# A hybrid SSD block on one core: two of the second norm's conditioning sums move from the scan stage into the output projection, and a chunk's own part is accumulated onto its decayed state output

## The chip, the cores and the metric

One core of a Trainium2 chip runs the whole kernel. The metric is the device time of one execution in microseconds (us); lower is better. The engines are TensorE (PE, with its weight loads as PEld), VectorE (DVE), ScalarE (ACT), GpSimd (POOL) and SyncE (SP), which issues all the transfers of this kernel from one in-order queue.

## The reference, cut to what matters

One layer of a diffusion backbone: a bidirectional Mamba-2 (SSD) mixer over 512 latent tokens that starts from the final state of 256 context tokens, then a convolutional gated FFN. Six conditioning vectors come from one vector `c` through `ada_w` (1024 x 6144): shift, scale and gate of the first norm, and the same of the second.

```python
sh1, sc1, g1, sh2, sc2, g2 = split(silu(c) @ ada_w[i] + ada_b[i], 6)
hl = rmsnorm(x, norm1_w[i]) * (1 + sc1) + sh1
oc, ol = mamba2_mixer(hc, hl, ...)
x = x + g1 * ol
x = x + g2 * conv_ffn(rmsnorm(x, norm2_w[i]) * (1 + sc2) + sh2, ...)
```

```python
# one direction of the mixer, per chunk of 128 tokens and head
y = (einsum("bcrls,bcsrp->bclrp", mix, xd)                       # the chunk's own part
     + einsum("bcln,bcrpn,bcrl->bclrp", cc, carried, exp(la_cs)))  # decayed state output
```

So `sh2` and `sc2` (parts 3 and 4 of the six) are needed only when the second norm's output is modulated, after the output projection; `g1` (part 2) is needed where that projection's result is added to `x`.

## The kernel before, in words

**Stages.** The kernel normalizes and transposes the input (until about 70 us), then works group by group over four groups of eight heads (the scan stage), then applies `w_out` (the output projection), the FFN's up projection with its convolution, and its down projection. All large weights are split into a high and a low part (`split`, line 94: ACT copies the high part, DVE subtracts it), and each product is three matmuls.

**The scan stage.** `ssm_group` (line 714) runs one group: the state passes (`advance`), and per chunk `mixing` (line 753), which loads decays (`R`), runs the DVE scan on them, adds the two directions into `M`, multiplies it with `cb`, and loads the decays to the chunk (`eb`). Per chunk two sorts of matmul follow: `pi`, the chunk's own part (eight fp32 matmuls of `xk` and `M`), and `pe`, the state output of either direction (four each). Five DVE instructions of 128x512 join them: `pe*eb` for both directions, their sum, the sum with `pi`, and the sum into `u`. `pi` and the two `pe` take one bank each of the PSUM pool `py`, which has three.

**What fills the gaps.** While group g is scanned, `blend` (line 931) interleaves "pieces" of other work in the code: the input projections of group g+1 (`proj_pieces`), gate projections with `w_z` (`gate_pieces`), and the conditioning sums (`ada_pieces`, line 843). A conditioning part has eight pieces; a piece loads 128 rows of `ada_w` (512 KB) and adds them, scaled by `silu(c)`, into a 128x1024 sum with one DVE instruction. `with_ada` puts one such piece behind each other piece, until the 24 pieces of parts 3, 4 and 2 are used up:

```python
ada = chain(ada_pieces(3, ada_acc, then=ada_to_cols), ada_pieces(4, ada_acc, then=ada_to_cols),
            ada_pieces(2, ada_acc, then=ada_bias))
```

`ada_to_cols` (line 866) sums the 128 partitions with eight small matmuls against `ones` (the tile `ada_c`); `ada_to_rows` (line 879) does so for `g1` in the output projection. All weight tiles, of `ada_w` too, go through one pool of three buffers (`wraw`, line 84); their high and low parts through another of three (`wsp`).

**The output projection.** `token_matmul` (line 969) takes 16 tiles of `w_out` (`raw_o`, split into `hi_o` and `lo_o`) against `u` (`uh`, `ul`) into eight PSUM banks (`o`); the last four tiles are kept, and for them the tokens are done block by block (i = 0 to 3). Behind a block come `add_and_norm` (line 1033: `ot`, the sum with `x`, the norm `xn`) and `modulated` (line 1048: transposes into the same banks, scale and shift into `h2hi` and `h2lo`). Three tiles of the FFN's up weights (`raw_a`, `raw_g`, `raw_a`) are loaded and split in advance.

**Order.** Outside the stretches that are held in program order, a scheduling layer places the instructions of each engine's queue; each engine then runs its queue in order.

Of the kernel before, what the change touches and what calls it, by code (L numbers as in the profile page):

```python
# [10 lines left out]
F32 = mybir.dt.float32  # L11
# [3 lines left out]
ALU = mybir.AluOpType  # L15
# [51 lines left out]
def hybrid_kernel(  # L67
# [646 lines left out]
    def ssm_group(g):  # L714
# [82 lines left out]
        for ch in range(NC):  # L797
            cs = slice(ch * P, (ch + 1) * P)
            M, eb = nxt
            pi = bank(py, f"pi{g}{ch}").rearrange("p (j l) -> p j l", l=P)  # L800
            for j in range(4):
                for q in range(2):
                    h = 2 * j + q
                    mm(pi[64 * q:64 * q + 64, j], xk[:, ch, h * HD:(h + 1) * HD], M[:, 4 * q + j])
            t = eb
            for dr, S in ((0, Sf), (1, Sb[ch])):
                pe = bank(py, f"pe{g}{ch}{dr}").rearrange("p (j l) -> p j l", l=P)
                for j in range(4):
                    mm(pe[:, j], S[:, j * P:(j + 1) * P], cT[:, cs])
                V.tensor_tensor(pe if dr else t[:, 0], pe, eb[:, dr], op=ALU.mult)  # L810

            V.tensor_tensor(t[:, 0], t[:, 0], pe, op=ALU.add)
            V.tensor_tensor(pi, pi, t[:, 0], op=ALU.add)
            us = u[:, 4 * g:4 * g + 4, cs]
            V.tensor_tensor(us, us, pi, op=ALU.add)
            if ch < NC - 1:
                nxt = mixing(ch + 1)
                yield
                Sf = advance(Sf, 0, ch, f"Sf{g}_{ch + 1}")
            yield  # L820
# [44 lines left out]

    def ada_to_cols(part, a):
        pc = bank(pj, f"ada_c{part}")
        for m in range(KD):
            mm(pc[:, m:m + 1], a[:, m * P:(m + 1) * P], ones)
        V.tensor_tensor(modc[:, part, :, 0], pc[:, :KD], prmB[:, KD * part:KD * part + KD], op=ALU.add)  # L870
        if part == 4:
            V.scalar_tensor_tensor(h2s, modc[:, 4, :, 0], 1.0, n2w, ALU.add, ALU.mult)
# [5 lines left out]

    def ada_to_rows(a, name):
        parts = split(a, name)  # L880
        for h in range(2):
# [22 lines left out]
    def with_ada(pieces):  # L904
        for p_ in pieces:
            yield p_
            yield from islice(ada, 1)

    ada = chain(ada_pieces(3, ada_acc, then=ada_to_cols), ada_pieces(4, ada_acc, then=ada_to_cols),
                ada_pieces(2, ada_acc, then=ada_bias))  # L910
    phases = [proj_pieces(0)] + [with_ada(p_) for p_ in (
        proj_pieces(1), proj_pieces(2), chain(proj_pieces(3), gate_pieces(0)),
        chain(gate_pieces(1), gate_pieces(2)), gate_pieces(3))] + [ada]
    ends = []
# [31 lines left out]
    finish_phase(0)  # L946
    for g, ratio in enumerate((0.6, 0.6, 0.9, 0.6)):
        blend(ssm_group(g), g + 1, ratio)
# [16 lines left out]
    h2hi = x2p.tile([P, KD, LAT], F32R, tag="h2hi", name="h2hi")  # L965
    h2lo = x2p.tile([P, KD, LAT], F32R, tag="h2lo", name="h2lo")
    Q.dma_start(x2, x.rearrange("(i p) d -> p i d", p=P))
# [49 lines left out]
    with tc.tile_pool(name="uo", bufs=5) as uo, tc.tile_pool(name="wlo", bufs=4) as wlast:  # L1017
# [11 lines left out]
        last_of = lambda: [wlast.tile([P, 1024], F32R, tag=n, name=f"{n}_last") for n in ("whi", "wlo")]  # L1029
        get_w = lambda k, last: wrows(w_out, k, f"o{k}", None, last_of if last else None)  # L1030
        xns = {}
# [45 lines left out]
        for i, o in token_matmul(acc8, 16, get_w, get_u, 3, 4, 512, up_ahead):  # L1077
            add_and_norm(i, o)
            if 0 < i < 3:
                modulated(i - 1, acc8[i - 1])  # L1080
# [20 lines left out]
    def gate2():  # L1101
        yield from stream(ada_pieces(5, g2r, True, ada_bias), 0)
        ada_to_rows(g2r, "g2b")
        yield
# [111 lines left out]
```

## Time and profile before

| | us |
|---|---|
| median of 3 runs | 971.22 (969.15 to 972.81) |
| the profiled execution's own time | 972.9 |
| its span, first to last instruction | 971.1 |
| TensorE busy in the span | 902.7 |
| VectorE busy in the span | 717.2 |

The span is what the views below divide; the profiled execution took 1.8 us more than its span, and lies within 0.2% of the median. "Busy" of TensorE is a sum over matmuls whose ends are modelled, so it includes the time that a matmul is stretched by a lower clock.

### The profile page before, as it was taken

The numbers are of one execution on the slowest core, as the hardware profiler recorded it, in microseconds if no ns is written. First come the engines' busy times: TensorE is split into PE (matmuls) and PEld (weight loads), VectorE is DVE, ScalarE is ACT, GpSimd is POOL, SyncE is SP. The second block draws the span as 40 slices with busy tenths as digits, with TensorE's granted clock in tenths as the row PEclk, the third lists the DMA queues.
The fourth block names the chain that finished last, engine by engine and source line by source line (L and its number), as shares of the span: only waits on it lengthen the run. The fifth ranks groups of instructions, "written<-read, shape, count | busy, mean of one in ns | idle before, by whom it ended". The sixth has DMA issues, their size and how long they took to land.

```text
span 971.1 us, 12065 instructions
## 1 busy us (share of the span) xinstructions
PE 902.7 (93%) x4595; PEld 736.8 (76%) x4595; DVE 717.2 (74%) x961; ACT 344.8 (36%) x523; POOL 301.6 (31%) x223
## 2 busy tenths in 40 slices
PE   7999868788889979899999999999989999999996
PEld 6688756666667767687888888888868888888885
DVE  5689989888977889657754457878898888843336
ACT  6463332222213322334344336444544333321223
POOL 2133249454535632414100004002400000453446
PEclk9999888899999999899999999999999999999998
DMA  9923364435554365533434350334534333323322
GB/s 313 292 57 101 109 145 119 112 94 155 169 144 120 98 184 141 141 88 104 135 121 140 109 152 1 112 112 148 161 107 120 87 107 92 105 87 92 104 65 87
DMA packets 137891, 119.70 MB, mean 123 GB/s; under 512 B 23245, under 2 KB 118249, under 8 KB 137833
## 3 DMA queue, kind: packets, MB, share of 16 engines
q1 hardware_dynamic: 137833, 118.93, 42.3%
q8 instruction: 36, 0.59, 0.3%
q14 instruction: 22, 0.18, 0.1%
HBM read 116.49 MB, written 2.43 MB: 122 GB/s over the span
## 4 chain that ended last, share of the span: by engine, by line
PE 51%; DVE 24%; DMA 12%; issue 9%; POOL 2%; ACT 2%; SPq 1%; DVEq 0%; ACTq 0%; POOLq 0%
PE d L59 12%; PE o L59 8%; PE pz L59 8%; PE pg L59 7%; PE pa L59 6%; DMA R<-da_d 5%; DMA adaw<-in_ada_w_dram 4%; DVE M L59 3%; DVE ada_acc L59 3%; DVE R L59 2%; DVE et L59 2%; PE pl_x L59 2%; DVE fc L59 2%; SPq L59 1%; DVE cv_lx L59 1%
## 5 line engine op out<-in xcount | busy, mean ns | idle before, releaser
L59 DVE SCALAR_TENSOR_TENSOR fc<-pa,prmC,fc 128x441 f32<-128x441 f32 (+2 forms) x176 | 121.4, 693 | 13.3 <-ACT fc L59 9.8
L59 POOL TENSOR_TENSOR raw_d<-raw_d,g2r 128x1024 f32<-128x1024 f32 x22 | 56.1, 2556 | 176.1 <-DMA raw_d<-in_ffn_w_down_dram 159.8
L59 PE MATMUL pa<-h2lo,hi_a 128*128 128x512 f32 (+1 forms) x192 | 71.5, 373 | 0.8 <-POOL h2lo L59 0.5
L59 PE MATMUL pa<-h2hi,lo_a 128*128 128x512 f32 (+1 forms) x192 | 71.5, 372 | 0.6 <-DVE lo_a L59 0.6
L59 PE MATMUL pa<-h2hi,hi_a 128*128 128x512 f32 (+1 forms) x192 | 71.5, 373 | 0.1
L59 PE MATMUL pg<-h2hi,lo_g 128*128 128x512 f32 (+1 forms) x184 | 70.1, 381 | 0.4 <-DVE lo_g L59 0.4
L59 PE MATMUL pg<-h2hi,hi_g 128*128 128x512 f32 (+1 forms) x184 | 70.1, 381 | 0.0
L59 PE MATMUL pg<-h2lo,hi_g 128*128 128x512 f32 (+1 forms) x184 | 69.9, 380 | 0.0
L59 DVE TENSOR_TENSOR lo_d<-raw_d,hi_d 128x1024 fp32r<-128x1024 f32 x18 | 34.2, 1902 | 42.9 <-ACT hi_d L59 42.9
L59 PE MATMUL pl_x<-hhi,hi_x 128*128 128x512 f32 x128 | 54.2, 425 | 4.0 <-DVE cv_cx L59 4.0
L59 POOL TENSOR_TENSOR M<-M,tok_m 64x512 f32<-64x512 f32 x32 | 41.9, 1310 | 51.1 <-DMA M<-em_d 43.2
L59 DVE TENSOR_TENSOR_SCAN R<-R,dg 128x1024 f32<-128x1024 f32 x16 | 40.2, 2516 | 23.7 <-DMA R<-da_d 17.2
L59 PE MATMUL pl_x<-hhi,lo_x 128*128 128x512 f32 x128 | 53.4, 419 | 0.0
L59 PE MATMUL pz<-hhi,lo_z 128*128 128x512 f32 x128 | 52.7, 412 | 0.0
L59 PE MATMUL pz<-hhi,hi_z 128*128 128x512 f32 x128 | 52.7, 412 | 0.0
L59 PE MATMUL pl_x<-hlo,hi_x 128*128 128x512 f32 x128 | 51.6, 405 | 0.0
L59 PE MATMUL pz<-hlo,hi_z 128*128 128x512 f32 x128 | 51.2, 400 | 0.0
L59 POOL TENSOR_TENSOR dg<-diag,tok_dt 128x1024 f32<-128x1024 f32 x16 | 34.4, 2148 | 42.7 <-DVE R L59 41.7
L59 POOL TENSOR_TENSOR xw<-xk,tok_w 128x512 f32<-128x512 f32 x24 | 35.1, 1468 | 34.1 <-PE ps_Sf L59 17.1
L59 PE MATMUL d<-lo_d,fhi 128*128 128x512 f32 x144 | 44.5, 389 | 0.0
L59 PE MATMUL d<-hi_d,flo 128*128 128x512 f32 x144 | 44.5, 389 | 0.0
L59 PE MATMUL d<-hi_d,fhi 128*128 128x512 f32 x144 | 43.6, 389 | 0.0
(339 smaller groups left out, 2410.6 us busy)
## 6 DMA issues: line engine op xcount, KB each, us to landing
adaw<-in_ada_w_dram SPq DMA_DIRECT2D x32, 512.0 KB, 3.8
raw_a<-in_ffn_w_up_dram SPq DMA_DIRECT2D x22, 512.0 KB, 4.6
raw_g<-in_ffn_w_up_dram SPq DMA_DIRECT2D x22, 512.0 KB, 4.0
raw_d<-in_ffn_w_down_dram SPq DMA_DIRECT2D x22, 512.0 KB, 3.7
adaw<-in_ada_w_dram SPq DMA_DIRECT2D x8, 1024.0 KB
raw_x<-in_ssm_w_in_dram SPq DMA_DIRECT2D x16, 512.0 KB, 3.9
R<-da_d SPq DMA_DIRECT2D x32, 256.0 KB, 4.4
eb<-e_d SPq DMA_DIRECT2D x32, 256.0 KB, 5.1
```

Of the source, the lines that this page charges most:

```text
L59: ins = f(*a, **kw)
```

## The change

Two things change. First, in a chunk the state outputs are multiplied by their decays before the chunk's own part is computed: the forward one in place in its PSUM bank, the backward one into `eb`; the eight `pi` matmuls then accumulate (`start=False`) onto the forward bank, and two DVE sums follow instead of three. A chunk takes two banks of `py` instead of three. Second, parts 3 and 4 leave the scan stage: their pieces are called from `get_w` of the output projection, one behind each `w_out` tile, into a buffer that `h2lo` takes over later, and `ada_to_cols` writes its columns into a bank of block 0 once block 1's matmuls are issued. Part 2's eight pieces move to the last group's scan, whose ratio rises from 0.6 to 1.2; the FFN's gate row (`gate2`) is split one piece earlier than it is multiplied.

```diff
-            pi = bank(py, f"pi{g}{ch}").rearrange("p (j l) -> p j l", l=P)
+            pes = []
+            for dr, S in ((0, Sf), (1, Sb[ch])):
+                pe = bank(py, f"pe{g}{ch}{dr}").rearrange("p (j l) -> p j l", l=P)
+                for j in range(4):
+                    mm(pe[:, j], S[:, j * P:(j + 1) * P], cT[:, cs], start=(j == 0))
+                V.tensor_tensor(eb[:, 1] if dr else pe, pe, eb[:, dr], op=ALU.mult)
+                pes.append(pe)
+            pi = pes[0]
             for j in range(4):
                 for q in range(2):
                     h = 2 * j + q
-                    mm(pi[64 * q:64 * q + 64, j], xk[:, ch, h * HD:(h + 1) * HD], M[:, 4 * q + j])
-            t = eb
-            for dr, S in ((0, Sf), (1, Sb[ch])):
-                pe = bank(py, f"pe{g}{ch}{dr}").rearrange("p (j l) -> p j l", l=P)
-                for j in range(4):
-                    mm(pe[:, j], S[:, j * P:(j + 1) * P], cT[:, cs])
-                V.tensor_tensor(pe if dr else t[:, 0], pe, eb[:, dr], op=ALU.mult)
-            V.tensor_tensor(t[:, 0], t[:, 0], pe, op=ALU.add)
-            V.tensor_tensor(pi, pi, t[:, 0], op=ALU.add)
+                    mm(pi[64 * q:64 * q + 64, j], xk[:, ch, h * HD:(h + 1) * HD], M[:, 4 * q + j], start=False)
+            V.tensor_tensor(pi, pi, eb[:, 1], op=ALU.add)
...
-    ada = chain(ada_pieces(3, ada_acc, then=ada_to_cols), ada_pieces(4, ada_acc, then=ada_to_cols),
-                ada_pieces(2, ada_acc, then=ada_bias))
-    phases = [proj_pieces(0)] + [with_ada(p_) for p_ in (
-        proj_pieces(1), proj_pieces(2), chain(proj_pieces(3), gate_pieces(0)),
-        chain(gate_pieces(1), gate_pieces(2)), gate_pieces(3))] + [ada]
+    ada = ada_pieces(2, ada_acc, then=ada_bias)
+    phases = [proj_pieces(0), proj_pieces(1), proj_pieces(2), chain(proj_pieces(3), gate_pieces(0)),
+              with_ada(chain(gate_pieces(1), gate_pieces(2))), with_ada(gate_pieces(3)), ada]
...
-    for g, ratio in enumerate((0.6, 0.6, 0.9, 0.6)):
+    for g, ratio in enumerate((0.6, 0.6, 0.9, 1.2)):
...
-    h2lo = x2p.tile([P, KD, LAT], F32R, tag="h2lo", name="h2lo")
+    ada34 = x2p.tile([P, 4, D], F32, tag="h2lo", name="ada34")
...
-        get_w = lambda k, last: wrows(w_out, k, f"o{k}", None, last_of if last else None)
+        mod2 = stream(chain(ada_pieces(3, ada34[:, 0]), ada_pieces(4, ada34[:, 1])), 0)
+        def get_w(k, last):
+            w = wrows(w_out, k, f"o{k}", None, last_of if last else None)
+            next(mod2, None)
+            return w
...
             add_and_norm(i, o)
+            if i == 1:
+                for part in (3, 4):
+                    ada_to_cols(part, ada34[:, part - 3], acc8[0][1][:, 32 * part:])
+                h2lo = x2p.tile([P, KD, LAT], F32R, tag="h2lo", name="h2lo")
             if 0 < i < 3:
                 modulated(i - 1, acc8[i - 1])
```

The engines' queues move in three places that matter. On VectorE, in the scan of the third group where its second chunk is prepared, the queue before holds five `ada_acc` instructions and the two small ones that end part 3 and 4 (`modc`, `h2s`):

```order
L59 TENSOR_TENSOR modc<-ada_c_2791,prmB 128x8
L59 TENSOR_SCALAR ada_acc<-adaw_2788,s_col 128x1024
L59 TENSOR_TENSOR M_2899<-M_2899,cb_2541 128x1024
L59 SCALAR_TENSOR_TENSOR R_3017<-R_3017,dg_3022 128x1024
L59 SCALAR_TENSOR_TENSOR h2s<-modc,prmA 128x8
L59 SCALAR_TENSOR_TENSOR ada_acc<-adaw_2916,s_col,ada_acc 128x1024
L59 SCALAR_TENSOR_TENSOR cv_cx_2865<-pc_x_2815,prmA,cv_cx_2865 128x255
L59 TENSOR_TENSOR Sb_0_2678<-Sb_0_2678,ps_Sb_0_2674 128x512
L59 SCALAR_TENSOR_TENSOR ada_acc<-adaw_3033,s_col,ada_acc 128x1024
L59 SCALAR_TENSOR_TENSOR cv_cx_2865<-pc_x_2815,prmA,cv_cx_2865 128x255
L59 SCALAR_TENSOR_TENSOR ada_acc<-adaw_3133,s_col,ada_acc 128x1024
```

At the same place (the third group's second and third chunk) the changed queue has only the scan's and the projections' own instructions:

```order
L59 TENSOR_TENSOR Sb_1_2600<-Sb_1_2600,ps_Sb_1_2596 128x512
L59 TENSOR_TENSOR pe_2742<-pe_2742,eb_2525 128x512
L59 SCALAR_TENSOR_TENSOR cv_lx_2737<-pl_x_2707,prmA,cv_lx_2737 128x511 x2
L59 TENSOR_TENSOR lo_c_2962<-raw_c_2781,hi_c_2961 128x1024
L59 SCALAR_TENSOR_TENSOR cv_cx_2837<-pc_x_2787,prmA,cv_cx_2837 128x255 x2
L59 TENSOR_TENSOR Sb_0_2673<-Sb_0_2673,ps_Sb_0_2669 128x512
L59 TENSOR_TENSOR M_2942<-R_2943 64x8x64 x2
L59 TENSOR_TENSOR M_2942<-M_2942,cb_2475 128x1024
L59 SCALAR_TENSOR_TENSOR R_3064<-R_3064,dg_3069 128x1024
```

What moved: the first `ada_acc` of the scan stage now stands in the last gate projections of the third group's scan, and eight are left there instead of 24.

On VectorE again, at the end of the output projection, ahead of the first block's `ot`, the queue before is:

```order
L59 TENSOR_TENSOR wlo_last<-raw_o_4513,whi_last 128x1024
L59 TENSOR_TENSOR lo_o_4472<-raw_o_4469,hi_o_4471 128x1024
L59 TENSOR_TENSOR wlo_last<-raw_o_4523,whi_last 128x1024
L59 SCALAR_TENSOR_TENSOR ul_4530<-u,prmA,uh_4529 128x512
L59 TENSOR_TENSOR wlo_last<-raw_o_4533,whi_last 128x1024
L59 TENSOR_TENSOR lo_a_4546<-raw_a_4543,hi_a_4545 128x1024
L59 SCALAR_TENSOR_TENSOR ul_4540<-u,prmA,uh_4539 128x512
L59 TENSOR_TENSOR lo_g_4552<-raw_g_4549,hi_g_4551 128x1024
L59 TENSOR_TENSOR lo_a_4558<-raw_a_4555,hi_a_4557 128x1024
L59 SCALAR_TENSOR_TENSOR ot_4585<-o_4087,rstd_87,ada_acc 128x512
```

and of the change:

```order
L59 TENSOR_TENSOR wlo_last<-raw_o_4451,whi_last 128x1024
L59 SCALAR_TENSOR_TENSOR ada_3966<-adaw_4457,s_col,ada_3966 128x1024
L59 TENSOR_TENSOR wlo_last<-raw_o_4464,whi_last 128x1024
L59 SCALAR_TENSOR_TENSOR ada_3966<-adaw_4470,s_col,ada_3966 128x1024
L59 SCALAR_TENSOR_TENSOR ul_4487<-u,prmA,uh_4486 128x512
L59 TENSOR_TENSOR wlo_last<-raw_o_4477,whi_last 128x1024
L59 SCALAR_TENSOR_TENSOR ada_3966<-adaw_4483,s_col,ada_3966 128x1024
L59 TENSOR_TENSOR lo_a_4493<-raw_a_4490,hi_a_4492 128x1024
L59 TENSOR_TENSOR lo_g_4499<-raw_g_4496,hi_g_4498 128x1024
L59 TENSOR_TENSOR lo_a_4505<-raw_a_4502,hi_a_4504 128x1024
L59 SCALAR_TENSOR_TENSOR ot_4532<-o_3986,rstd_87,ada_acc 128x512
```

What moved: the conditioning sums (`ada_3966`) stand between the splits of the last `w_out` tiles, and the three splits of the up weights come closer to `ot`.

On TensorE, behind the last matmul of block 1 (bank `o_4090` before, `o_3989` in the change), the queue before goes on with:

```order
L59 MATMUL o_4090<-whi_last,ul_4540 128x512
L59 MATMUL o_4087<-ident,xn_4591 128x128 x4
L59 MATMUL o_4088<-ident,xn_4591 128x128 x4
L59 MATMUL o_4091<-whi_last,uh_4509 128x512
L59 MATMUL o_4092<-whi_last,uh_4509 128x512
```

and the changed one with:

```order
L59 MATMUL o_3989<-whi_last,ul_4487 128x512
L59 MATMUL o_3987<-ones,ada_3966 128x1 x16
L59 MATMUL o_3986<-ident,xn_4538 128x128 x4
L59 MATMUL o_3987<-ident,xn_4538 128x128 x4
L59 MATMUL o_3990<-whi_last,uh_4447 128x512
L59 MATMUL o_3991<-whi_last,uh_4447 128x512
```

What moved: sixteen small matmuls of the column sums stand ahead of block 0's transposes and of block 2.

## Rows read from the trace of the kernel before

**Rows 1.** Windows: length, then PE, PEld, DVE, ACT, POOL busy, clock, DMA share, GB/s.

```profile
70.00:130.00 60.00, 52.66 (x284) 46.09 (x283) 58.01 (x97) 21.55 (x36) 16.91 (x22) 0.91 0.37 103
...
280.00:330.00 50.00, 45.88 (x280) 37.17 (x279) 35.51 (x48) 18.83 (x31) 20.87 (x17) 0.97 0.43 118
...
70.00:404.00 334.00, 285.72 (x1596) 229.57 (x1594) 287.92 (x341) 96.89 (x159) 158.53 (x115) 0.93 0.49 131
...
404.00:503.50 99.50, 99.50 (x502) 79.44 (x501) 65.71 (x81) 37.33 (x58) 21.75 (x17) 0.98 0.35 100
...
503.50:583.00 79.50, 79.50 (x360) 65.92 (x359) 37.85 (x50) 31.03 (x41) 2.20 (x2) 1.00 0.47 147
```

**Rows 2.** Waits of PE from 130 to 404 us: total, times, longest.

```profile
PE pi L59 <- DVE M L59: 8.8, 2, 6.9
PE pe L59 <- DVE u L59: 8.0, 4, 4.0
PE ps_Sb L59 <- DVE Sb L59: 6.2, 2, 5.9
PE pi L59 <- DVE eb L59: 4.4, 2, 3.3
```

**Rows 3.** DVE by line and form, 70 to 130 us: busy, mean ns, idle before.

```profile
L59 DVE SCALAR_TENSOR_TENSOR ada_acc<-adaw,s_col,ada_acc 128x1024 f32<-128x1024 f32 x4 | 7.3, 1830 | 0.0
```

**Rows 4.** The same view, 130 to 404 us.

```profile
L59 DVE TENSOR_TENSOR_SCAN R<-R,dg 128x1024 f32<-128x1024 f32 x15 | 37.1, 2476 | 21.7 <-DMA R<-da_d 15.2 <-DMA M<-em_d 3.3 <-POOL xw L59 2.4
L59 DVE TENSOR_TENSOR M<-R 64x512 f32<-64x512 f32 x28 | 32.1, 1146 | 0.3
L59 DVE SCALAR_TENSOR_TENSOR ada_acc<-adaw,s_col,ada_acc 128x1024 f32<-128x1024 f32 x17 | 31.0, 1821 | 4.0 <-DMA adaw<-in_ada_w_dram 4.0
...
L59 DVE TENSOR_TENSOR eb<-eb,pe 128x512 f32<-128x512 f32 x12 | 8.1, 675 | 0.1
...
L59 DVE SCALAR_TENSOR_TENSOR ada_acc<-ident,prmB,ada_acc 128x128 f32<-128x128 f32 x8 | 3.0, 446 | 0.0
...
L59 DVE TENSOR_SCALAR ada_acc<-adaw,s_col 128x1024 f32<-128x1024 f32 x2 | 2.1, 1060 | 0.0
```

**Rows 5.** Instructions on the tile ada_acc: ns min/median/max, first and last start.

```profile
L59 DVE SCALAR_TENSOR_TENSOR ada_acc<-adaw,s_col,ada_acc x21: 1250/1627/3518, 84.1 to 370.9; 128x1024 f32<-128x1024 f32 x21
```

**Rows 6.** PE by line and form, 130 to 404 us: busy, mean ns, idle before.

```profile
L59 PE MATMUL ada_c<-ones,ada_acc 128*128 128x1 f32 x32 | 3.9, 235 | 0.0
```

**Rows 7.** Transfers: issues, KB each, median us to landing.

```profile
adaw<-in_ada_w_dram SPq DMA_DIRECT2D x32, 512.0 KB, 3.8
...
R<-da_d SPq DMA_DIRECT2D x32, 256.0 KB, 4.4
...
raw_o<-in_ssm_w_out_dram SPq DMA_DIRECT2D x16, 512.0 KB, 4.8
...
raw_b<-in_ssm_w_in_dram SPq DMA_DIRECT2D x4, 512.0 KB, 7.2
```

**Rows 8.** Instructions on the tile raw_o: its landing times.

```profile
DMA to landing us min/median/max: 3.4/4.8/6.1
```

**Rows 9.** Timeline of DVE in the output projection, one tile of twelve.

```profile
527.40 0.75 DVE L59 SCALAR_TENSOR_TENSOR ul<-u,prmA,uh 128x512 fp32r<-128x512 f32 x1 [3.27 <-ACT uh L59]
528.34 1.23 DVE L59 TENSOR_TENSOR lo_o<-raw_o,hi_o 128x1024 fp32r<-128x1024 f32 x1 [0.19 <-ACT hi_o L59]
532.84 0.75 DVE L59 SCALAR_TENSOR_TENSOR ul<-u,prmA,uh 128x512 fp32r<-128x512 f32 x1 [3.27 <-ACT uh L59]
```

**Rows 10.** Timeline of DVE at the first block's end.

```profile
571.70 1.23 DVE L59 TENSOR_TENSOR lo_a<-raw_a,hi_a 128x1024 fp32r<-128x1024 f32 x1 [3.71 <-ACT hi_a L59]
575.83 1.41 DVE L59 SCALAR_TENSOR_TENSOR ot<-o,rstd,ada_acc 128x512 f32<-128x512 f32 x2 [2.90 <-PE o L59]
...
580.40 0.81 DVE L59 TENSOR_SCALAR xn<-x,rp_s,rp_t 128x1024 f32<-128x1024 f32 x1
```

**Rows 11.** Timeline of PE at block 1's end.

```profile
581.36 1.06 PE L59 MATMUL o<-ident,xn 128*128 128x128 f32 x8
```

More of the change, by code (lines that the diff above doesn't have):

```diff
@@ L864, in ada_pieces, with ada_to_cols @@
             yield partial(load, k), partial(run, k=k)
-    def ada_to_cols(part, a):
-        pc = bank(pj, f"ada_c{part}")
+    def ada_to_cols(part, a, pc):
         for m in range(KD):
@@ L877, in ada_bias, with ada_to_rows @@
             V.scalar_tensor_tensor(a[:, s], ident, prmB[:, KD * part + m:KD * part + m + 1], a[:, s], ALU.mult, ALU.add)
-    def ada_to_rows(a, name):
-        parts = split(a, name)
+    def ada_to_rows(a, name, parts=None):
+        parts = parts or split(a, name)
         for h in range(2):
@@ L1102, in gate2 @@
         yield from stream(ada_pieces(5, g2r, True, ada_bias), 0)
-        ada_to_rows(g2r, "g2b")
+        parts = split(g2r, "g2b")
+        yield
+        ada_to_rows(g2r, "g2b", parts)
         yield
```

## The prediction, made before the changed kernel was run

> **What bounds the kernel now.** I read the windows first, since the busy shares of the whole span average over stages with different limits. In [rows 1] the reader should compare TensorE (the first number behind the length) with VectorE (the third). From 404 to 503.5 us, the last gate projections, TensorE is busy all 99.5 us, and so it is from 503.5 to 583, the output projection (79.50 of 79.5), where VectorE has 37.85. There nothing but TensorE's own work sets the time, and VectorE work is free as long as it comes in time. From 70 to 404 us, the scan of the first three groups, it is otherwise: of 334 us TensorE has 285.72 (85.5%) and VectorE 287.92 (86.2%), and the granted clock is 0.93 on average, so part of TensorE's busy time is matmuls at 1.2 instead of 2.4 GHz. TensorE is idle there for 334 - 285.7 = 48.3 us.
>
> Next, whom it waits for: the longest waits [rows 2] all end with a VectorE instruction (`M`, `u`, `Sb`, `eb`), 27.4 us in four rows. That is a queue that runs late, and the lines of VectorE [rows 3, 4] tell with what: the scan itself, the additions into `M`, and then `ada_acc`, the conditioning sums, which nothing in this stage needs.
>
> **What leaves the scan stage.** All 24 sums leave the stretch from 70 to 404: 16 (parts 3 and 4) go to the output projection, eight (part 2) to the last group. On VectorE that is 7.3 [rows 3] and 31.0 + 2.1 + 3.0 us [rows 4] (the 17 sums, the first products of a part, and the bias that ends part 2). The three chunks' sums become two: one of the five 128x512 instructions goes in each of the 12 chunks that end in this stretch, 8.1 us [rows 4]; the other four lie beside a busy TensorE and count nothing. Together 51.5 us, so VectorE goes from 287.9 to 236.4. TensorE loses the column sums, 3.9 us [rows 6], to 281.8.
>
> How much of 51.5 becomes time? Not all: the idle time of TensorE that can close is 48.3. I take the answer from two stretches of this trace. Over all of 70 to 404 VectorE is busy 86.2% and TensorE 85.5%; from 280 to 330 VectorE is busy 35.51 of 50 (71.0%) and TensorE 45.88 (91.8%) [rows 1]. That is 0.414 points of TensorE for each point of VectorE. With a length T, 281.8/T must lie on that line at 236.4/T: T = (281.8 + 0.414 x 236.4) / (0.918 + 0.414 x 0.71) = 313 us. VectorE is then busy 75% and TensorE 90%, between the two stretches. The clock was 0.97 in the better one against 0.93 overall; halfway, 0.95, matmuls cost about 5 us less, and T becomes 309: a gain of 25. The bounds are 0 (each wait finds another cause) and 48 of idle time, with some 10 more if the clock also rises by the whole 0.04.
>
> **The chunk's new order.** A chunk took three banks of a pool of three, so the next chunk's matmuls waited until `u` and `eb` had read them: 8.0 and 4.4 us [rows 2]. With two banks per chunk the next forward output finds a free bank; I count half, 6 us. Against it stands a new wait: the `pi` matmuls come behind the product in place, and what is queued behind them on TensorE (the next projection) waits too. In the changed queue up to 24 other matmuls lie between, but not always; one 0.7 us instruction in a quarter of 16 chunks is about 3. Net 3, between -11 (all 16 wait for one full instruction) and +12. The scan stage so gains **28 us**.
>
> **What the last group gets.** Part 2's eight sums and its bias, 8 x 1.63 (the median in [rows 5]) + 3.0 = 16 us, go where VectorE has 65.71 of 99.5 us busy and TensorE is the limit [rows 1]: nothing, as long as their eight extra loads through the three `wraw` buffers don't hold up the `raw_z` tiles behind them in the queue. If the cover is gone they cost up to 16.
>
> **What the output projection gets.** Sixteen sums of 1.25 us (the minimum in [rows 5], as GpSimd has 2.20 us here [rows 1]) are 20 us on an engine that is busy 37.85 of 79.5. A step of the loop takes 5.44 us (from one `ul` to the next [rows 9]) and has 0.75 + 1.23 us of VectorE; with a sum it has 3.2. So the arithmetic is hidden. Three things are not:
> the column sums, 3.9 us [rows 6], stand on TensorE between block 1 and block 0's transposes, which before followed at once (581.36 [rows 11]): 3.9 us in full, where before they had partly filled idle time.
> The second half of those transposes reuses the columns' bank, so it waits for VectorE to read them, behind block 1's `ot`: 0.5 us.
> The loads. Before, the third up tile was split by 572.9 and VectorE then idled 2.90 us until `ot` [rows 10]. Now each of the last four steps has a sum as well, on the same queue and buffers, and the three up tiles, whose splits stand ahead of `ot`, follow the last sum. Four transfers more in the line, with 3.8 us each to landing [rows 7], overlapped threefold, are 5 us later and each adds 1.25 of sum: I put `ot` at 0 to 8 us late, 4 in the middle. `ot` leads to `xn` (575.83 to 581.2 [rows 10]), and in turn to block 0's transposes, so it counts in full.
> Sum 8.4, say **8 us**, between 4 and 16.
>
> **The sum.** 971.1 - 28 + 8 = 951.1 for the span. The profiled execution took 972.9 with that span, the runs a median of 971.2; a gain of 20 puts the median at **951 us**, -2.1%.
>
> A row and a rule differ on one point. The same sum takes 1.25 to 3.52 us [rows 5], and the mean in the scan stage is 1.82 [rows 4]. The Trainium skill (SBUF — State Buffer, Who interferes with whom) says that a VectorE instruction with two SBUF inputs and a GpSimd instruction that reads SBUF lock one port pair against each other, whoever comes first; then the time above 1.25 is GpSimd's, and the instructions that stay will meet it instead. By that rule the 17 sums give back 17 x 1.25 = 21.3 instead of 31.0, VectorE stays at 246, T is 3 us longer, and the time 954; the trace agrees with the spread, but no row here shows who inherits the wait. I keep the row and hold 954 inside the range.
>
> **The rivals.**
> *The loads of the output projection decide (slower).* In its second half the sums use one buffer over and over: a load of a sum's tile starts when the sum before is done, and the next `w_out` tile stands behind it in the queue. The cycle is landing + 1.25. With 3.8 [rows 7] it is 5.05 and fits into a step of 5.44; with raw_o's median 4.8 it is 6.05, 0.6 too long, which about two steps of lead (11 us) cover. At 6.1, the longest landing in this stage [rows 8], it loses 16 x 1.9 = 31, less 11 of lead; at 7.2, what the first `raw_b` tiles took under load [rows 7], 16 x 3.0 = 48 less 11, so 37 more: 988. From 6.1 the whole gain is gone, from 6.4 it is slower by over 0.5%. For it: the bytes of this stage nearly double. Against: it moves 147 GB/s [rows 1] at those 4.8 us, and the median adaw load is quicker.
> *The waits only change their name (no change).* The chunk's chain of loads stays: `R` has one buffer, so a chunk is load 4.4 [rows 7] + scan 2.5 + two additions of 1.15 [rows 4] = 9.2 us; 21.7 us of VectorE idle stand before the scans already. Against: 12 chunks of 9.2 are 110 of 334 us, so the chain has slack. If it, with GpSimd's part, lets only 12 of 28 through: 971 - 12 + 8 = 967; with 8 through, 971.
> *The clock stays up (faster still).* If the gaps close far enough that the 0.93 becomes 0.97 and the idle time falls to 5% of the stretch, 272/0.95 = 286, a gain of 48: 971 - 48 + 8 = 931.
>
> **Chances.** My forecast, a net gain of 10 to 30 us (941 to 961): 0.58. The clock, 925 to 941: 0.12. Waits that partly change their name: 0.18, of which 961 to 966 has 0.08 and within 0.5% (966 to 976, about what a measurement of this kernel can tell from no change) has 0.10. Loads, over 976: 0.12. Faster by over 0.5%: 0.58 + 0.12 + 0.08 = 0.78. The range 934 to 969 leaves out about half of the clock's case (0.05) and the upper cases above 969 (0.15).
>
> **What would show it.** Right: from 70 us to the start of the last gate projections some 28 us less, TensorE about 90% busy and VectorE about 75% there, the waits for `u` and `eb` halved, the clock above 0.93; the output projection some 8 us longer, with a gap of TensorE before block 0's transposes and `ot` behind a late `lo_a`. Wrong: gaps of TensorE in every step of the output projection with `raw_o` as the releaser (the loads), or as many us of waits in the scan, now for `pe`, `R` or GpSimd's `xw` (renamed), or TensorE idle in the last group on `lo_z`.

## The result, and the profile after

The changed kernel takes 980.95 us (median of 4 runs, 978.24 to 982.47), the kernel before 970.52 beside it: a ratio of 1.0102 with a 95% interval of 1.0069 to 1.0135. It is 1.0% slower, where 2.1% faster was predicted and the range ended at 969.

The profiled execution took 979.59 us with a span of 977.8, 6.7 more than before (the medians are 10.4 apart: this execution lies below its median, that of the kernel before above its own). I cut both traces at the same three events: the first z projection (a gate projection with `w_z`), the last one, and the first matmul of the up-projection; the stretch between the last two is called the output projection. The kernel before, in the columns of [rows 1]:

```profile
130.00:379.20 249.20, 212.21 (x1203) 167.49 (x1203) 210.39 (x223) 67.52 (x111) 130.78 (x86) 0.93 0.51 138
379.20:503.00 123.80, 119.85 (x610) 95.06 (x609) 85.24 (x103) 45.11 (x69) 32.59 (x25) 0.97 0.39 105
503.00:594.80 91.80, 91.18 (x414) 75.42 (x414) 47.83 (x71) 39.05 (x63) 8.43 (x7) 1.00 0.42 129
```

The changed kernel:

```profile
70.00:130.00 60.00, 54.22 (x294) 46.56 (x294) 50.73 (x91) 22.21 (x37) 18.46 (x23) 0.94 0.33 78
130.00:346.20 216.20, 195.04 (x1133) 154.85 (x1132) 161.03 (x175) 68.28 (x112) 109.52 (x77) 0.96 0.38 99
346.20:492.50 146.30, 129.64 (x646) 101.41 (x645) 104.71 (x120) 43.84 (x68) 47.88 (x31) 0.94 0.47 131
492.50:601.40 108.90, 99.09 (x436) 81.28 (x435) 65.44 (x91) 39.86 (x63) 7.95 (x7) 0.94 0.58 184
```

Three things are to be seen. The first z projection starts 33 us earlier (379.2 to 346.2). The stretch from there to the last z projection is 22.5 us longer, and TensorE, idle for 4.0 us in it before, is idle for 16.7 (12.6 of them among the last group's matmuls, 3.9 on the split of the first `w_out` tile). The output projection is 17.1 us longer (91.8 to 108.9), and TensorE idle for 9.8 in it, where it was 0.6. So 10.5 of the 33 us are left when the output projection begins, and they are lost there; behind it the two kernels take the same.

The waits of TensorE in the scan, the view of [rows 2] from 120 to 400 us, for the changed kernel (total, times, longest):

```profile
PE sc L59 <- POOL xw L59: 9.5, 4, 6.9
PE pe L59 <- DVE pe L59: 6.5, 4, 3.1
PE pe L59 <- DVE Sf L59: 4.2, 1, 4.2
PE ps_Sb L59 <- POOL xw L59: 4.2, 3, 3.4
```

The bank waits of [rows 2] (for `u` and `eb`, 12.4 us) and those for `M` are gone, and others have their place: 13.7 us for GpSimd's `xw` (3.5 before, up to 404 us), 6.5 for the new product in place. Over all of 70 us to the last z projection TensorE is idle for 433.4 - 385.1 = 48.3 us before and 422.7 - 379.1 = 43.6 after: the idle time hardly closed, it moved.

The output projection's loss stands in the timeline of TensorE (start, duration, in brackets the idle time before and its releaser):

```profile
555.45 0.74 PE L59 MATMUL o<-lo_o,uh 128*128 128x512 f32 x2 [1.54 <-DVE lo_o L59]
565.46 0.73 PE L59 MATMUL o<-whi_last,uh 128*128 128x512 f32 x2 [0.61 <-ACT whi_last L59]
566.72 0.74 PE L59 MATMUL o<-wlo_last,uh 128*128 128x512 f32 x2 [0.53 <-DVE wlo_last L59]
...
577.24 3.57 PE L59 MATMUL o<-ones,ada 128*128 128x1 f32 x16 [3.84 <-DVE ot L59]
583.87 3.57 PE L59 MATMUL o<-ones,ada 128*128 128x1 f32 x16 [3.05 <-DVE modc L59]
587.30 1.95 PE L59 MATMUL o<-ident,xn 128*128 128x128 f32 x8
```

Block 1 ends at 573.4, 8 us earlier than before (581.36 [rows 11]), but block 0's transposes start 5.9 us later (587.30). Between lie some 14 us: 3.84 of wait for `ot`, 3.57 for part 3's columns (eight matmuls, which the trace has as 16), 3.05 of wait for VectorE to read them, 3.57 for part 4's. The other gaps in the stage are 2.9 us. The columns run at a granted clock of 0.50, 1.2 instead of 2.4 GHz; from 570 to 577 us, almost to the end of the first of these waits, it was 0.98:

```profile
577.00:588.00 11.00, 7.71 (x36) 7.62 (x37) 6.93 (x20) 3.26 (x10) 2.19 (x2) 0.50 0.22 62
```

The `ot` is late on VectorE:

```profile
570.66 1.23 DVE L59 TENSOR_TENSOR lo_a<-raw_a,hi_a 128x1024 fp32r<-128x1024 f32 x1 [2.05 <-ACT hi_a L59]
572.70 1.22 DVE L59 TENSOR_TENSOR lo_g<-raw_g,hi_g 128x1024 fp32r<-128x1024 f32 x1 [0.81 <-ACT hi_g L59]
574.64 1.22 DVE L59 TENSOR_TENSOR lo_a<-raw_a,hi_a 128x1024 fp32r<-128x1024 f32 x1 [0.72 <-ACT hi_a L59]
575.79 1.40 DVE L59 SCALAR_TENSOR_TENSOR ot<-o,rstd,ada_acc 128x512 f32<-128x512 f32 x2
```

It starts when it did before (575.83 [rows 10]), but now follows the third up tile at once, where it waited 2.90 us for TensorE. And the up tiles are issued late, behind the sums' tiles, which share the three buffers. SyncE's issues:

```profile
540.07 0.33 SPq L59 DMA_DIRECT2D raw_o<-in_ssm_w_out_dram  x1
543.59 0.33 SPq L59 DMA_DIRECT2D adaw<-in_ada_w_dram  x1
...
564.46 0.38 SPq L59 DMA_DIRECT2D raw_a<-in_ffn_w_up_dram  x1
```

Ten tiles leave in the 24.4 us between the first and the last of these rows, 2.44 us each. With three buffers in turn that makes, as an estimate, 7.3 us for a buffer's round (load, ScalarE's copy, VectorE's subtraction or sum, the next issue).

### The profile page after: what moved, and what is told of

It reads as the page before. It is cut to its first block, busy times and chain, and to the rows that moved or that the text cites. A ratio compares the mean times of both kernels' runs of the same rounds, so it can differ in the third digit from the quotient of the medians.

```text
span 977.8 us, 12047 instructions
## 1 busy us (share of the span) xinstructions
PE 905.5 (93%) x4595; PEld 737.4 (75%) x4595; DVE 697.4 (71%) x945; ACT 346.4 (35%) x523; POOL 298.5 (31%) x223
## 3 DMA queue, kind: packets, MB, share of 16 engines
q1 hardware_dynamic: 137833, 118.93, 41.9%
## 4 chain that ended last, share of the span: by engine, by line
PE 50%; DVE 22%; DMA 13%; issue 9%; ACT 3%; POOL 2%; SPq 1%; DVEq 0%; ACTq 0%; POOLq 0%
PE d L59 12%; PE pg L59 7%; PE o L59 7%; PE pa L59 6%; PE pz L59 5%; DMA R<-da_d 5%; DMA adaw<-in_ada_w_dram 4%; PE pe L59 3%; PE pl_x L59 3%; DVE M L59 3%; DVE et L59 2%; DMA eb<-e_d 2%; DVE R L59 2%; DVE fc L59 1%; DMA raw_o<-in_ssm_w_out_dram 1%
## 5 line engine op out<-in xcount | busy, mean ns | idle before, releaser
L59 DVE SCALAR_TENSOR_TENSOR fc<-pa,prmC,fc 128x441 f32<-128x441 f32 (+2 forms) x176 | 121.3, 692 | 13.3 <-ACT fc L59 9.9
L59 POOL TENSOR_TENSOR M<-M,tok_m 64x512 f32<-64x512 f32 x32 | 39.1, 1223 | 52.5 <-DMA M<-em_d 46.9
L59 PE MATMUL pl_x<-hhi,hi_x 128*128 128x512 f32 x128 | 51.7, 405 | 0.0
L59 PE MATMUL pz<-hhi,lo_z 128*128 128x512 f32 x128 | 51.1, 399 | 0.0
L59 POOL TENSOR_TENSOR xw<-xk,tok_w 128x512 f32<-128x512 f32 x24 | 37.2, 1558 | 32.8 <-ACT xk L59 16.7
```

Of the source, the lines that this page charges most:

```text
L59: ins = f(*a, **kw)
```

## The experiments

Each was timed in five rounds beside the kernel before. "End of z" is the end of the last z projection, "idle" TensorE's idle time and "VectorE" its busy time from 70 us to there, all from one profiled execution; its own time may lie up to 3.7 us off the median. The kernel before came to medians of 970.5 to 972.8 in these rounds, so a difference of some 2 us between two runs is not told from none. Groups are counted from 0, as in the code: the last is group 3.

| run | us | ratio to before (95%) | end of z | idle | VectorE |
|---|---|---|---|---|---|
| before | 970.5 to 972.8 | | 503.4 | 48.3 | 353.6 |
| after | 980.95 | 1.0102 (1.0069 to 1.0135) | 492.7 | 43.6 | 316.5 |
| e1_chunk_alone | 971.8 | 0.9992 (0.9976 to 1.0008) | 503.5 | 50.9 | 345.4 |
| e2_sums_alone | 979.37 | 1.0086 (1.0061 to 1.0111) | 492.1 | 47.2 | 325.0 |
| e3_own_buffers | 968.68 | 0.9956 (0.9938 to 0.9973) | 492.7 | 41.6 | 315.5 |
| e4_no_columns | 975.1 | 1.0043 (1.0024 to 1.0061) | 493.2 | 43.9 | 316.5 |
| e5_part2_early | 966.24 | 0.9944 (0.9925 to 0.9963) | 491.8 | 41.5 | 318.3 |
| e6_ratio_06 | 969.13 | 0.9977 (0.9963 to 0.9992) | 492.8 | 44.3 | 314.7 |
| e7_no_part2 | 965.52 | 0.9941 (0.9923 to 0.996) | 489.5 | 40.4 | 307.9 |
| e8_two_R | 969.98 | 0.9982 (0.9967 to 0.9996) | 493.4 | 44.3 | 313.5 |
| e9_xw_vector | 981.15 | 1.0096 (1.0071 to 1.012) | 503.6 | 51.1 | 342.0 |
| e10_best_xw | 971.37 | 0.9992 (0.9976 to 1.0007) | 494.8 | 44.3 | 347.7 |
| e11_m_vector | 975.28 | 1.0045 (1.0025 to 1.0065) | 501.6 | 49.7 | 340.1 |
| e12_resident_sums | 970.53 | 0.9989 (0.9974 to 1.0003) | 496.9 | 46.0 | 341.9 |
| e13_columns_back | 970.57 | 0.999 (0.9975 to 1.0006) | 500.4 | 43.4 | 315.0 |
| e14_loads_back | 964.8 | 0.9939 (0.9916 to 0.9962) | 490.3 | 41.9 | 324.8 |
| e15_sums_and_loads | 978.27 | 1.005 (1.0035 to 1.0065) | 500.6 | 52.1 | 344.5 |
| e16_all_back | 978.84 | 1.0051 (1.0033 to 1.0069) | 500.7 | 49.4 | 346.5 |
| e17_loads_beside_sums | 964.98 | 0.9925 (0.9907 to 0.9943) | 492.7 | 39.9 | 345.2 |
| e18_old_chunk | 966.08 | 0.994 (0.9921 to 0.9958) | 485.1 | 38.4 | 331.6 |

**Which half of the change.** e1 puts the chunk's new lines into the kernel before; e2 is the changed kernel with the chunk's old lines.

> The kernel before with nothing but the chunk's new order (product in place, pi matmuls onto it, two sums instead of three); all 24 conditioning sums stay where they were. Theory S (the scan of a group goes at the pace of its own chain of loads, scans and GpSimd products; taking VectorE work away only lets projections run earlier): within 5 us of the kernel before, 966 to 975 us. Rival C (the new product ahead of the pi matmuls costs what the sums gave back: the waits for pe, Sf and xw, 24 us in the changed kernel, come from it): slower, 978 us or more, with the waits of TensorE for pe and xw as in the changed kernel.

> The changed kernel with the chunk's three sums and three banks as before; the conditioning sums are moved. Theory S: the same as the changed kernel within 5 us, 976 to 986 us: z projections end near 493 and the output projection is 17 us longer than before. Rival C (the chunk's order ate the gain): the scan stage keeps the predicted 28 us, the z projections end near 475, and the time is about 971 - 28 + 17 = 960 us.

The chunk alone changes nothing, and the sums alone give the changed kernel's time and the same end of z. Rival C falls. That the waits for `pe` and `xw` stand in e1 too (7.9 and 16.4 us), without costing time, shows that such rows are no prices. In e2 group 2's first scan is at 260.8 us (275.4 in the changed kernel), and z ends at the same 492.

**The output projection.** e3 gives the sixteen sums' tiles two buffers of their own; e4 leaves the column sums out.

```diff
-            w = wraw.tile([P, 1024], F32, tag="wraw", name=f"adaw_{part}{k}")
+            w = (pool or wraw).tile([P, 1024], F32, tag="wraw", name=f"adaw_{part}{k}")
...
+... tc.tile_pool(name="aw2", bufs=2) as aw2:
-        mod2 = stream(chain(ada_pieces(3, ada34[:, 0]), ada_pieces(4, ada34[:, 1])), 0)
+        mod2 = stream(chain(ada_pieces(3, ada34[:, 0], pool=aw2), ada_pieces(4, ada34[:, 1], pool=aw2)), 0)
```

> The changed kernel with two buffers of their own for the tiles of the sixteen sums in the output projection; w_out and the up tiles have the three wraw buffers to themselves again. Theory L (the 35 tiles of this stage go three at a time through wraw, 7 to 8 us a round trip, so the up tiles and block 0's ot behind them come 8 us late): the stage falls from 109 to about 97 us, ot starts at block 0's end, the gaps on lo_o and whi_last go, and the time is 967 to 971 us. Rival K (the column sums and their waits on the bank decide, whatever the loads do): 14 us stay between block 1 and block 0's transposes, and the time stays at 977 to 981 us.

```diff
-                    ada_to_cols(part, ada34[:, part - 3], acc8[0][1][:, 32 * part:])
+                    V.tensor_copy(modc[:, part, :, 0], ada34[:, part - 3, :KD])
```

> The changed kernel without the column sums: modc takes eight numbers of the sums' tile instead (that part of the computation is left out); the sixteen sums and their loads stay. Theory L: block 0's ot still comes at about 575.8, and its xn, for which the transposes wait, at 581, so of the 14 us between block 1 and the transposes 8 stay: 6 us less than the changed kernel, about 975 us. Rival K: the 14 us go, about 967 us.

Both came out as theory L has it. (e3 gives the stage two buffers more and keeps the sums' tiles out of the others' way; which of the two counts was not separated.) With the own buffers the stage of e3 is

```profile
492.50:589.60 97.10, 96.11 (x436) 79.81 (x435) 65.75 (x91) 39.01 (x63) 7.97 (x7) 0.96 0.59 195
```

97.1 us instead of 108.9: 11.8 of the 12.3 us that e3 gains. Its `ot` waits for TensorE again, and the columns' part is 5.1 us instead of 14.0 (569.18 to 574.28):

```profile
563.72 1.41 DVE L59 SCALAR_TENSOR_TENSOR ot<-o,rstd,ada_acc 128x512 f32<-128x512 f32 x2 [1.72 <-PE o L59]
```

```profile
569.18 1.84 PE L59 MATMUL o<-ones,ada 128*128 128x1 f32 x16
571.94 2.48 PE L59 MATMUL o<-ones,ada 128*128 128x1 f32 x16 [0.92 <-DVE modc L59]
574.28 1.95 PE L59 MATMUL o<-ident,xn 128*128 128x128 f32 x8
```

The first of the two sets runs at a granted clock of 1.00 (569 to 573.2 us), the second into a fall to 0.50 (573.4 to 580); over both it is 0.85:

```profile
569.00:575.00 6.00, 5.08 (x38) 4.96 (x37) 4.10 (x13) 1.63 (x5) 1.27 (x1) 0.85 0.00 0
```

Without column sums (e4) the transposes stand where the sum said, at 582.64, behind block 0's late `xn`, and 5.9 us are won, not 14:

```profile
582.64 1.94 PE L59 MATMUL o<-ident,xn 128*128 128x128 f32 x8 [6.34 <-DVE xn L59]
```

**The last group, and the scan's own chain.** All on e3. e5 puts part 2's sums among the projections of groups 1 to 3, with ratio 0.6; e6 sets the ratio alone; e7 leaves seven of part 2's sums out, with ratio 0.6; e8 gives `R` two buffers.

```diff
-    phases = [proj_pieces(0), proj_pieces(1), proj_pieces(2), chain(proj_pieces(3), gate_pieces(0)),
-              with_ada(chain(gate_pieces(1), gate_pieces(2))), with_ada(gate_pieces(3)), ada]
+    phases = [proj_pieces(0), with_ada(proj_pieces(1)), with_ada(proj_pieces(2)), with_ada(chain(proj_pieces(3), gate_pieces(0))),
+              chain(gate_pieces(1), gate_pieces(2)), gate_pieces(3), ada]
-    for g, ratio in enumerate((0.6, 0.6, 0.9, 1.2)):
+    for g, ratio in enumerate((0.6, 0.6, 0.9, 0.6)):
```

> The kernel with two own buffers for the output projection's sums (968.7 us), and part 2's eight sums put back among the projections of the first three groups, the last group's ratio back at 0.6. Theory P (in the last group the sums stand in VectorE's queue before their tiles have landed, 14 us of waits for adaw, and hold the scan behind them, so the gain of the first groups is lost there): the z projections end some 10 us earlier, near 482, and the time is 956 to 962 us. Theory R (the scan of each group, the last one too, goes at the pace of its own loads of R and of GpSimd, whatever else is queued): 966 to 971 us.

> The kernel with two own buffers, the last group's ratio at 0.6 instead of 1.2: half as many z projections and sums between the steps of the last scan, the rest behind it. Theory P: fewer sums in the scan's way, but also fewer matmuls beside it: 964 to 969 us. Theory R: the last scan is as long and has less beside it, so some 7 z projections of 5 us are left over behind it where there were two or three: slower, 975 us or more.

```diff
-    ada = ada_pieces(2, ada_acc, then=ada_bias)
+    ada = islice(ada_pieces(2, ada_acc), 1)
```

> The kernel with two own buffers and only the first of part 2's eight sums (seven sums and their loads are left out), ratio 0.6, so that as many z projections stand beside the last scan as with sums at 1.2. The price of part 2 in the last group. Theory P: 14 us of waits and 11 us of VectorE's work go from the last scan, about 955 us. Theory R: 966 to 971 us.

```diff
-            R = sp.tile([P, 2, HPG, BL], F32, tag="R", name=f"R{g}{ch}", bufs=1)
+            R = sp.tile([P, 2, HPG, BL], F32, tag="R", name=f"R{g}{ch}", bufs=2)
```

> The kernel with two own buffers, and two buffers for R instead of one, so that the next chunk's decays can be loaded before the additions of this chunk have read the first. Theory R: the 22 to 25 us that VectorE waits for R's loads fall by more than half, the steps of the scan come earlier, and the time is 950 to 960 us. Theory P: the waits for R go, but what follows waits for eb's loads, GpSimd or adaw instead: 965 to 970 us.

Theory P falls: by the medians, part 2 early gains 2 us, part 2 left out 3. Theory R gets no support: with two `R` the time is the same, and with the ratio at 0.6 it is too, where it asked for 975 or more. The test with two `R` is a weak one, though: VectorE's waits for `R`'s loads fell from 21.8 to 18.2 us only (130 to 480 us), not by more than half. e5, e7 and e8 have 40 to 44 us of idle time.

**GpSimd.** e9 moves the products `xw` to VectorE (on e3), e10 the same on e5, e11 the product into `M` (on e3).

```diff
-        G.tensor_tensor(
+        V.tensor_tensor(
             heads(t), heads(xk),
             ej(tokcol(tok_w, dr, ch, g)), op=ALU.mult)
```

> The kernel with two own buffers (968.7 us), with all the products xw, GpSimd's since the kernel before, on VectorE. Theory G (what paces the scan now is GpSimd's queue: TensorE's longest waits there are for xw, 15 us): these waits go, the steps of the scan move up, the z projections end near 480, and the time is 950 to 960 us. Theory N (no engine is the bound: a group is a chain of loads, GpSimd, VectorE, ScalarE and TensorE, one behind the other, and a link that gets faster is followed by a wait for the next; VectorE with some 17 us more makes other links slower): 964 to 972 us, and TensorE idle for 40 to 48 us between 70 us and the end of the z projections as in every run so far.

> The same move of xw to VectorE in the kernel with part 2's sums among the first three groups (966.2 us). Theory G: 948 to 957 us. Theory N: 962 to 970 us.

> The kernel with two own buffers, with GpSimd's other product of a chunk, the one into M (32 of 1.2 us), on VectorE instead; xw stays on GpSimd. Theory G, since xw stands behind M in GpSimd's queue: 952 to 962 us. Theory N: 966 to 974 us.

All three are slower than their own base, by 12.5, 5.1 and 6.6 us; theory G falls, and N had expected too little. The `xw` instruction itself is quicker on VectorE (the 24 of the latent tokens take 1013 ns in the mean in e9, 1390 on GpSimd in e3), but TensorE waits 15.2 us for it there as well (`sc`, four waits): it comes no earlier.

**What a moved sum consists of.** The changed kernel and e3 end z some 10 us before the kernel before; which part of a moved sum is worth these 10 us? Its VectorE time, its load, its column sums, each put back alone on e3, then together; these come in addition to the sums in the output projection. e14 to e17 also have part 2 early and ratio 0.6, so their nearest base is e5, not e3.

```diff
+            if g:
+                src = dl[:, None, :].broadcast_to([P, 2, LAT])
...
+                    V.scalar_tensor_tensor(acc2, src, s_col[:, 1:2], acc2, ALU.mult, ALU.add)
```

> The kernel with two own buffers (968.7 us) with 18 sums of the same size more on VectorE, one behind each projection of groups 1 to 3, on data that are in SBUF already (their result is not used): VectorE's work of the conditioning sums is back in the scan of the first three groups, without their loads and without their column sums. Theory D (VectorE's time is what the scan stage waits for, at the half microsecond for each that the prediction took from the two windows): 18 x 1.8 = 32 us, so 16 us slower, about 984 us. Theory N (TensorE's idle time there stays as it is, whoever is named): 968 to 974 us, with TensorE idle for 40 to 50 us between 70 us and the end of the z projections.

```diff
+            if g in (1, 2) and nm == "c":
+                rows = u[:, 4 * g:4 * g + 2].rearrange("p k l -> p (k l)")
+                ada_to_cols(2 + g, rows, bank(pj, f"ada_c{2 + g}"))
```

> The kernel with two own buffers (968.7 us), with two sets of column sums on TensorE back among the projections of groups 1 and 2, taken from data in SBUF (the result is overwritten later, so the same values come out). Part by part the 10.7 us that the changed kernel is ahead at the end of the z projections are looked for: 18 sums on VectorE alone gave 4. If the column sums are the rest: the z projections end 4 to 7 us later than 492.7, and the time is 972 to 976 us. If they fill idle time: 968 to 970 us.

```diff
+        def use(w, k):
+            V.tensor_copy(ada_acc[:, k:k + 1], w[:, 0:1])
...
+    ada = chain(loads_alone(3), loads_alone(4), ada_pieces(2, ada_acc, then=ada_bias))
```

> The kernel with two own buffers, with sixteen loads of 512 KB through the wraw buffers back among the pieces of the first groups, each read by one copy of a single column (the sums themselves stay in the output projection, so these loads are in addition, and part 2's sums follow them as in the kernel before; ratio 0.6). If the loads (their place in the queue and the three buffers) are what the sums cost the scan stage: the z projections end 5 to 8 us later than 492.7, and the time is 973 to 978 us. If not: 966 to 970 us.

e12 costs 1.9 us, e13 1.9 (medians; its profiled execution was 3.7 us above its median). e14 is 3.9 us faster than e3, but 1.4 faster than e5, its nearest base, which is not clear of noise. Alone, none of the three is the 10 us. Together:

```diff
+    ada = chain(ada_pieces(3, ada_acc), ada_pieces(4, ada_acc), ada_pieces(2, ada_acc, then=ada_bias))
```

> The kernel with two own buffers, with parts 3 and 4 in the first groups as in the kernel before (sixteen loads and the sums that wait for them, part 2 behind), in addition to those in the output projection; no column sums. VectorE's own time gave 2 us, the loads alone nothing. If only the two together count (a sum that waits for its tile holds the scan behind it in VectorE's queue): z projections end near 500 and the time is 973 to 978 us. If each part is worth what it was alone: 966 to 971 us.

e16 is the same with `then=cols`, which issues the column sums.

> The same with the column sums back as well, so that the scan stage carries all that the kernel before had there, and the output projection all that the changed kernel has. The z projections should end at 503 as in the kernel before; with the output projection of the own buffers, 97 us, the time is 977 us. If the parts are worth what they were alone, 969 to 973 us, and then the 10.5 us have another source.

Sums with their loads cost 9.6 us over e3 (12.0 over e5), the column sums 0.6 more. e17 joins e14's loads and e12's sums, so that none of the 18 sums waits for a load (part 2's eight still do, and a copy of one column, 0.15 us, waits for each of the sixteen tiles):

> The kernel with the sixteen extra loads (964.8 us: each read by one copy of a single column) and, beside them, the 18 sums on data in SBUF of the run with resident sums: the same loads and the same VectorE work as with sums and loads (978.3 us), but no sum waits for a load. If it is the wait of a sum for its tile that costs the 10 us: 964 to 970 us. If loads and VectorE work together do, whatever waits for what: 974 to 980 us.

It takes 964.98 us. Here are the windows of e15 and of e17:

```profile
70.00:500.60 430.60, 378.49 (x2069) 301.61 (x2068) 344.54 (x402) 133.51 (x215) 184.43 (x131) 0.96 0.47 127
```

```profile
70.00:492.70 422.70, 382.82 (x2068) 306.37 (x2068) 345.19 (x419) 134.09 (x214) 182.93 (x131) 0.95 0.47 130
```

VectorE is busy for the same 345 us, the DMA moves the same, and e17 is 13.3 us faster (7.9 at the end of z). So the amount of VectorE's work is not the bound of this stage; a sum that is tied to its tile costs, the same sum and the same load apart do not. The two also differ in place: e17 has no sums before 143.8 us, and its first scan starts at 131.8 instead of 138.4. But e5, with its first scan at 138.2, is as fast as 966.2, so an early first scan is not what counts. What the tie does is not shown. It may be the wait in VectorE's queue, the tile's buffer, which a sum of 1.25 us or more holds longer than a copy, or the sums' place in the queue; e15 with buffers of their own for the sums' tiles in the scan stage would test the second, and was not run. Against the first speak VectorE's own waits for `adaw` (total, times, longest) in e15, in e16, which takes as long, in e14, which is one of the two quickest, and in e17:

```profile
DVE ada_acc L59 <- DMA adaw<-in_ada_w_dram: 13.2, 10, 3.3
```

```profile
DVE ada_acc L59 <- DMA adaw<-in_ada_w_dram: 5.7, 7, 1.6
```

```profile
DVE ada_acc L59 <- DMA adaw<-in_ada_w_dram: 20.7, 11, 4.7
```

```profile
DVE ada_acc L59 <- DMA adaw<-in_ada_w_dram: 7.8, 7, 5.2
```

They don't follow the time. Nor is the loss in one place. The last group's first scan in e15, e16 and e17:

```profile
380.94 2.28 DVE L59 TENSOR_TENSOR_SCAN R<-R,dg 128x1024 f32<-128x1024 f32 x1
```

```profile
369.98 2.29 DVE L59 TENSOR_TENSOR_SCAN R<-R,dg 128x1024 f32<-128x1024 f32 x1 [1.15 <-DMA R<-da_d]
```

```profile
372.90 2.29 DVE L59 TENSOR_TENSOR_SCAN R<-R,dg 128x1024 f32<-128x1024 f32 x1
```

e15 has lost its 8 us by then; e16 is ahead of e17 there and ends z 8.0 us later all the same.

**The chunk again.** e18 takes the chunk's new lines out of e5.

> The kernel with own buffers and part 2 in the first groups (966.2 us) with the three sums and three banks of a chunk as before. The chunk's new order alone was worth nothing on the kernel before (971.8). If it is worth nothing here either: 963 to 969 us. If it helps once the sums are out of the scan, by the 8 us of VectorE that it takes away: 970 us or more.

966.08 against 966.24: the chunk's new order is worth nothing here either. Its profile has the bank waits back (`tx` for `eb` 7.0 us, `pi` for `M` 7.6) and VectorE at 331.6 us instead of 318.3, and the time is the same. Its z projections end 6.7 us earlier in the profile (485.1), of which 1.1 are lost in the output projection and 3.1 behind it; the medians show nothing of the rest.

e5, e14, e17 and e18 compute the whole layer and are faster than both kernels, by 0.6 to 0.75% against the one before; e14 and e17 carry work without use. What can be kept is e5 or e18.

## Why the prediction was wrong, point by point

**The scan stage's 28 us: the step that failed.** It is the one that asks "How much of 51.5 becomes time?" and answers with a line through two stretches, "0.414 points of TensorE for each point of VectorE". The shares themselves came as it said: from 70 to 346.2 us TensorE is busy 90.2% (forecast 90) and VectorE 76.7% (75). But the idle time was not closed. By the line T was 313 us with 281.8 of TensorE, 31 of idle time instead of 48.3: 17 us were to close, and 4.7 did (48.3 to 43.6). TensorE runs the projections between the scan's steps; with fewer sums among the pieces they go earlier (the first z projection by 33 us), while a group's first scan does not. The first scan of groups 2 and 3, in the timeline of VectorE before:

```profile
274.29 2.29 DVE L59 TENSOR_TENSOR_SCAN R<-R,dg 128x1024 f32<-128x1024 f32 x1 [0.17 <-DMA R<-da_d]
...
359.25 2.29 DVE L59 TENSOR_TENSOR_SCAN R<-R,dg 128x1024 f32<-128x1024 f32 x1 [2.20 <-DMA R<-da_d]
```

and after:

```profile
275.40 2.28 DVE L59 TENSOR_TENSOR_SCAN R<-R,dg 128x1024 f32<-128x1024 f32 x1
...
356.32 2.29 DVE L59 TENSOR_TENSOR_SCAN R<-R,dg 128x1024 f32<-128x1024 f32 x1 [2.59 <-DMA R<-da_d]
```

The projections that TensorE has done early are then missing as cover, that is as work to fill the last group's gaps; the traces fit that, but no run tests it by itself, and e2, whose group 2 does start its first scan 14 us earlier, ends z no sooner. The sum stopped at the stage's border, at 404 us, and took the last group as still 100% busy behind it. To the end of z, 10.7 us are left of 28: 4.7 of idle time and 6.0 of TensorE's busy time (385.1 to 379.1), where the sum had 8.9 for the column sums and the clock. What the runs put in the line's place: a microsecond of VectorE has no fixed price here. 18 resident sums, 26 us of VectorE, move the time by 2 (e12), where the line asks for about half; beside loads, and not tied to them, they cost nothing against e5 (e17); tied to their loads, 10 to 12 (e15); and the 26 us that `xw` adds, in the scan's own chain, 12.5 (e9). What sets the scan stage's time in the end stays open.

**+3 for the chunk.** Measured 0, within the stated -11 to +12. The bank waits did go, and the new wait behind the product did come (6.5 us).

**The last group, 0.** As a price for part 2 this was nearly right (2 to 3 us by the medians, e5 and e7). That TensorE would stay busy there was wrong, with or without part 2.

**The output projection, 8 us.** Measured 17.1, just over the upper bound of 16. The terms: the column sums (3.9 us for 32 records in their row) took 7.1, at a granted clock of 0.50 from 577 to 588 us; the second bank wait came to 3.05, since the read of part 3's columns stands behind block 1's `ot` and an addition (0.5 was put there for one); `ot` came 12.1 us later than with own buffers (575.79 against 563.72 in e3), where 0 to 8 were put, and 3.84 of that reached TensorE as a direct wait (4 forecast); the gaps ahead of block 1's end, mostly on `lo_o`, `whi_last` and `wlo_last`, 2.9, were put at 0. The mis-sized term is that of the loads, 4 in the sum: e3 takes 11.8 us out of the stage, and with own buffers 5.3 of the 17.1 stay.

**The rival that came.** "The loads of the output projection decide" had the right place, and the sign. Its price was formed from landing plus 1.25 us and asked for landings of 6.1 to lose the gain; the median `raw_o` landing is 4.7 here. What a tile holds a buffer for is the round of 7.3 us, and the test was not each step of the loop but the end: three up tiles at the end of the line, with `ot` behind them, against a TensorE that comes 10 us earlier. Its own sign, gaps in every step with `raw_o` as releaser, did not appear.

**"Waits only change their name"** is what the scan stage did: it gave 10.7 of 28, near that rival's 12. With its 8 us for the output projection that is some 968; the 9 us more there make it slower than before. Its reason, the chain of loads of `R`, is not shown (e8).

**The clock** rose from 0.93 to 0.96 in the first groups as told, and fell to 0.94 in the last group and the output projection, from 0.97 and 1.00, where there had been hardly a gap before.

**The rule weighed there** (the Trainium skill, SBUF — State Buffer, Who interferes with whom) would have moved the time by 3 us by way of VectorE's busy time. As e12 shows what 26 us of that are worth, its 3 can't be told from nothing here; the spread on which it bears is seen again in e15 (sums of 1254 to 2771 ns).

## What to carry to other kernels

Before you turn idle time into a gain, follow it to the next fixed event: if the work that filled the gaps can run ahead, relief in one stage can be given back where that cover is missing (33 us early at the first z projection, 10.5 at the last). Price a moved load by how long it holds its buffer (here 7.3 us, not the 4.7 to landing) and by what stands at the end of the line. Price a wait by an experiment with the same work and no dependence, since the rows of waits did not follow the time here: 13.2 and 5.7 us in two runs of 978 us, 20.7 and 7.8 in two of 965.

## What was not expected of the hardware

The eight matmuls of a column sum (16 records) took 3.57 us in the changed kernel, where the granted clock is 0.50 (577 to 588 us), 1.2 of 2.4 GHz, and 1.84 and 2.48 us in e3 (0.85 from 569 to 575). In the changed kernel the fall comes at the end of 3.84 us without work; in e4, without column sums, it comes within 6.34 us without work (576.3 to 582.64 us; the clock is 0.50 from 580.1 to 586.8); in e3 it follows the first column sum, 0.92 us without work and the start of the second; the kernel before has none of these and a clock of 1.00 there (573 to 594.8). So the time without work seems to have cost twice here: of the output projection's 17.1 us, 9.2 are idle time and 7.9 more busy time, of which the columns would be 4.3 at e3's lengths.

Sixteen loads of 512 KB that nobody needs cost nothing: e14 takes 964.8 us, e5 without them 966.24, at 130 instead of 110 GB/s from 70 us to the end of z.
